# Later due times in a planned instruction order, and 64-row matmul operands padded to 128 rows

## The chip, the cores and the metric

The kernel runs on one core of one Trainium2 chip. The metric is device time in microseconds (us), the median over the runs shown. The core has a matmul engine (TensorE; PE in the rows, its weight loads PEld), VectorE (DVE), ScalarE (ACT), GpSimd (POOL) and SyncE (SP), which issues nearly all DMAs here. Each engine takes its instructions in the order in which the program lists them, and a waiting instruction holds up those behind it on its engine.

## The reference, cut

One step of an encoder with two layers, for a prompt of 512 rows and a sample of 64 rows with a model width of 2048. The two are laid side by side as T = 576 rows: four and a half blocks of 128. Layer 0 has two branches, A and B, that share one input projection; layer 1 is an attention with two softmax maps per head. Everything is float32.

```python
def ab_layer(x, ...):                                    # layer 0
    u, v_a, g_a, h_b, g_b = split(x @ w_in)
    v_n = layer_norm(v_a)                                # branch A
    out_a = u * spatial_gate(v_n, a_ws, a_bs) * silu(g_a)      # lower-triangular mixing in chunks of 128 rows
    hs = h_b + (prev - h_b) * b_mu                       # branch B; prev = h_b one row earlier
    r, k, v, wl, al = split(hs)
    decay = exp(-exp(-softplus(-(b_w0 + tanh(wl) @ b_w2)) - 0.5))
    a = sigmoid(b_a0 + al @ b_a2)
    ...
    wkv_new, y = rwkv7_scan(wkv0, r, decay, k_mod, v, kk, a)   # 16 heads of 64
    out_b = (group_norm(y) + sum(r * k_mod * b_rk) * v) * silu(g_b)
    return layer_norm(ALPHA * x + concat([out_a, out_b]) @ w_out)

def step(s, inp):                                        # rwkv7_scan, one row
    s_kk = einsum('bhvk,bhk->bhv', s, kk_t)
    s = s * w_t - s_kk * (kk_t * a_t)^T + v_t * k_t^T    # state of 64 x 64 per head
    return s, einsum('bhvk,bhk->bhv', s, r_t)

def c_layer(x, k_cache, v_cache, ...):                   # layer 1; the sample reads 512 cached rows too
    q, k, v, g = split(x @ w_in)
    attn = softmax(q1 k1) - lam * softmax(q2 k2)
    return layer_norm(ALPHA * x + (sub_norm(attn @ v) * silu(g)) @ w_out)
```

## The kernel before, in words

**Projections.** Most of the matmul work is `x @ w_in` and `x @ w_out` of both layers, cut into units of 128 output columns (`run_unit`). Numbers are split into a high and a low part, so that each product takes three matmuls (L280 to L282): high weights by high x, high weights by low x, low weights by high x. `x_...` is a tile of x, `wh` and `wl` are the parts of the weights, `p` the result. Weights come in by DMAs of 256 KB on the SP queue (L207, `w_dma`); ACT makes `wh` (L221), DVE or POOL `wl` (L223).

**Side work.** All else is written as generators that run beside the projections. A planner, `Flow`, walks through the program before it is built and counts an assumed time: each triple of projection matmuls adds 3 x columns / 2.35 ns (327 ns for 256 columns, 408 ns for 320). A generator yields two numbers, the time that its matmuls take and a delay; it is called again at the first triple at which the planner's time has passed the delay:

```python
    def step(self, h):
            pe_ns, lat = next(h[1])
            self.t += pe_ns
            h[0] = self.t + lat
    def tick(self, ns):
        self.t += ns
        for h in list(self.sides):
            if h in self.sides and h[0] <= self.t:
                self.step(h)
```

So a delay decides how many projection matmuls stand between two pieces of side work. It sets an order for every engine and no time: at run time an instruction waits for its operands where it stands.

**Branch B** runs in 8 groups of two heads (groups 1 to 8 in the text, `g` = 0 to 7 in the code). `prepare` makes the decays (`sig`, L692, cumulated L716, `EP` and `EN`), `av` (L698), `rn` (L726, L727) and `rkm` (L735). `rwkv` makes `AR` and `KB` (DVE, L749 to L753) and their products per chunk of 64 rows (L773, `MM`), and turns the group's old state `st` (L796). The blocks on the diagonal of `MM` are inverted on DVE in 72 small tiles (L813): they reach this form by a store and a load (`ND`, `NT`), and the result `XX` and its transposed form go back by a store (`XD`, L820 and L821) and two loads each into `X16` and `V16` (L825; X and V in the rows). `stepmm` (L647) takes `X16` first, then `V16`, and builds the remaining inverse `ZB`.

**The chain of states.** The state goes through the 9 chunks in 8 steps (the first takes two chunks at once). One step, a link, is: PE L860 (`cq` from `VU`, `MM`), ACT copies `R1` (L864), PE L867 (`R1`, `ZB`), DVE copies to `VU` (L870), PE L873 (`VU`, `KB`), DVE makes the next `VU` (L881 or L883), which the next L860 needs. After the chain come the outputs `yq` (L896, L900) and `normalise` (L913 to L941), which scales them with `L162` out of the transposes of `yd` (L929).

**64-row operands.** The sample makes the fifth block of rows half full. Where a matmul or a transpose contracts over the rows of such a block, or over one head's 64, it takes 64 rows of the array: `to_features` (L189) for x, for the norm between the layers (`z`) and for the attention's output (`O`); `vn` (L471), `av` (L698), `sig` (L716), `st` (L796), and in layer 1 `aTs` (L1370) and `ovs` (L1381).

Of the kernel before, what the change touches and what calls it, by code (L numbers as in the profile page):

```python
# [10 lines left out]
F32 = mybir.dt.float32  # L11
# [106 lines left out]
def hybrid_step(ctx: ExitStack, tc: tile.TileContext, a: dict, o: list):  # L118
# [64 lines left out]
    def to_features(src, part, f0, m0=0):  # L183

        q = ps("tf")
        c = 0
        for m in MP[part]:
            n = rows(m)
            pe.transpose(q[:, c:c + n], src[:n, m - m0, f0:f0 + 128], ident[:n, :n])  # L189
            c += n  # L190
        return q[:, 0:c]

# [201 lines left out]
    with tc.tile_pool(name="xld", bufs=4) as xlp:  # L394
# [49 lines left out]
        def gated(j):  # L444
            vt = ap_.tile([128, 5, 128], F32, tag="at", name="vn")
            gb = ap_.tile([128, 3, 128], F32, name="gb")
            sp.dma_start(out=vt[:, 0:4, :], in_=VD[j][:, 0:4, :])
            sp.dma_start(out=vt[:64, 4, :], in_=VD[j][:64, 4, :])
# [18 lines left out]
            for ms in MP:  # L467
                q = ps()
                for i, m in enumerate(ms):
                    n = rows(m)  # L470
                    pe.matmul(q[:, 128 * i:128 * i + n], vt[:n, m, :], WST[:n, g, 0:n], start=True, stop=True)  # L471
                c0 = 128 * ms[0]
                dve.tensor_tensor(out=gt[:, c0:c0 + 256].rearrange("p (m t) -> p m t", m=2),
                                  in0=q[:, 0:256].rearrange("p (m t) -> p m t", m=2),
                                  in1=gb[:, 2:3, :].to_broadcast([128, 2, 128]), op=ALU.add)
                if len(ms) == 3:
                    dve.tensor_tensor(out=gt[:, 512:576], in0=q[:, 256:320], in1=gb[:, 2, 0:64], op=ALU.add)
                yield 110 * len(ms), 0
# [92 lines left out]
    WA = lp.tile([128, T], F32, name="WA")  # L571
    TW = lp.tile([65, T], F32, name="TW")
    pool.memset(TW[64:65, :], 1.0)

    def ev_shift(j, part, p):
# [81 lines left out]
    def rwkv_loads(g):  # L657
        w2 = r2p.tile([128, 2, 128], F32, name="w2")
        sp.dma_start(out=w2[0:64, 0, :], in_=a["ab_b_w2"][0, :, 128 * g:128 * g + 128])
        sp.dma_start(out=w2[64:65, 0, :], in_=a["ab_b_w0"][0:1, 128 * g:128 * g + 128])  # L660
        sp.dma_start(out=w2[64:128, 1, :], in_=a["ab_b_a2"][0, :, 128 * g:128 * g + 128])
        st = r2p.tile([64, 2, 64], F32, name="st")
        sp.dma_start(out=st, in_=a["state_b_wkv"][0, 0, 2 * g:2 * g + 2].rearrange("h v k -> v h k"))
        LOADS[g] = (w2, st)
# [17 lines left out]
    def prepare(g):  # L682
# [6 lines left out]
        for m in range(5):  # L689
            n = rows(m)  # L690
            q = q0[:, 128 * m:128 * m + 128] if m < 4 else q1[:64, 0:128]
            pe.matmul(q, TW[:, 128 * m:128 * m + n], w2[0:65, 0, :], start=True, stop=True)  # L692
        act.activation(out=sig[:, 0:4, :], in_=q0.rearrange("p (m f) -> p m f", m=4), func=AF.Sigmoid)
        act.activation(out=sig[:64, 4, :], in_=q1[:64, 0:128], func=AF.Sigmoid)
        av = fp.tile([128, T], F32, tag="f", name="av")
        for c0, c1 in TP:
            q = ps()
            pe.matmul(q[:, 0:c1 - c0], w2[64:128, 1, :], WA[64:128, c0:c1], start=True, stop=True)  # L698
            act.activation(out=av[:, c0:c1], in_=q[:, 0:c1 - c0], func=AF.Sigmoid, bias=A0[:, g:g + 1])
# [11 lines left out]
        for ms, ch in (((0, 1), (0, 4)), ((2, 3, 4), (4, 9))):  # L711
            q = ps()
            for i, m in enumerate(ms):
                n = rows(m)
# [24 lines left out]
    def rwkv(g):  # L739
# [117 lines left out]
        for cs in ((8, 0), (1,), (2,), (3,), (4,), (5,), (6,), (7,)):  # L857
# [16 lines left out]
            for c in cs:  # L874
# [155 lines left out]
    def z_tiles(zp, part, n=4):  # L1030
# [154 lines left out]
    def ev_v(hd, e, part, p):  # L1185
# [82 lines left out]
    def core(hd):  # L1268
# [74 lines left out]
        def sample_scores():  # L1343
            q0, q1 = ps("s0"), ps("s1")
            for j in range(2):
                pj = slice(64 * j, 64 * j + 64)
                pe.matmul(q0[pj, :], qT[j][:, 128:192], kcT[:, j, :], start=True, stop=True)
                pe.matmul(q1[pj, 0:64], qT[j][:, 128:192], kT[j][:, 512:576], start=True, stop=True)
            Pt = a2.tile([128, T], F32, tag="P", name="Ps")
            mx = a2.tile([128, 2], F32, name="mx")  # L1350
# [14 lines left out]
        def sample_values():  # L1365
            Pt, rr = st.pop("s")
            q = ps("aTs")
            for m in range(5):
                n = rows(m)
                pe.matmul(q[:n, 64 * m:64 * m + 64], Pt[:, 128 * m:128 * m + n], rr, start=True, stop=True)  # L1370
            aT = a1.tile([128, 2, 512], F32R, tag="aT", name="aTs")
            for n, cs in ((128, slice(0, 256)), (64, slice(256, 320))):
                dve.tensor_copy(aT[:n, 0, cs], q[:n, cs])
                dve.tensor_tensor(out=aT[:n, 1, cs], in0=q[:n, cs], in1=aT[:n, 0, cs].bitcast(F32), op=ALU.subtract)
            yield 5 * 150, 2800
            q = ps("ovs")
# [284 lines left out]
```

## Time and profile before

| | |
|---|---|
| runs | 2517.45, 2525.48 and 2527.79 us; median 2525.48 |
| profiled execution | 2536.78 us; span 2535.0 us, mean granted clock of TensorE 0.987 |
| busy, share of the span | PE 2433.9 us (96%), PEld 92%, DVE 52%, ACT 36%, POOL 20% |
| DMA | 281.71 MB, 111 GB/s over the span |
| chain that ended last | PE 81%, DVE 8%, DMA 8%, issue 2%, ACT 1%, SP's queue 1% |

The chain that ended last follows the work back from the last instruction to whatever released each step. "Busy" of a matmul includes time in which it stands in the pipeline behind another, so 96% does not say that 96% of the span is full use. A granted clock of 1.00 is 2.4 GHz and 0.50 is 1.2 GHz. Layer 0 is the first 1100 us of the span, roughly; branch B's groups lie in it.

### The profile page before, as it was taken

To read this page: it belongs to the slowest core of one execution; us is meant where nothing else is said; L and a number is where in the kernel's file an instruction comes from. 1 tells how busy PE (TensorE), PEld (TensorE's weight loads), DVE (VectorE), ACT (ScalarE), POOL (GpSimd) and SP (SyncE) were. 2 spreads that over 40 slices of the span, in tenths; PEclk is the share of its full clock that TensorE was granted. 3 is DMA by queue.
4 is the path that set the end of the run, shared out by engine and by line. 5 is a ranking of instruction groups with operands and counts; after the bars stand their busy time and mean duration, and the time that the engine had idled before them with its cause. 6 is when DMAs were issued, how large, how long until landed. Compare 5 with 4: busy or idle time off the path is not lost.

```text
span 2535.0 us, 48231 instructions
## 1 busy us (share of the span) xinstructions
PE 2433.9 (96%) x19033; PEld 2335.1 (92%) x19033; DVE 1327.7 (52%) x3030; ACT 904.1 (36%) x1827; POOL 517.2 (20%) x618
## 2 busy tenths in 40 slices
PE   8999898989898999999999999999999999999898
PEld 8988897979797988899999999999999999999897
DVE  4357465657474666556655434243333334356665
ACT  3424242414233231244434424243433433243342
POOL 1221212222221221121215121212021211213411
PEclk9999999999999999999999999999999999999998
DMA  6252424243342514267656242323233323337664
GB/s 178 71 96 60 80 70 78 75 72 86 57 91 54 104 48 90 91 214 220 189 159 181 84 120 81 102 85 107 85 103 89 97 88 98 102 92 231 186 184 148
DMA packets 528051, 281.71 MB, mean 111 GB/s; under 512 B 81288, under 2 KB 520010, under 8 KB 527818
## 3 DMA queue, kind: packets, MB, share of 16 engines
q1 hardware_dynamic: 527824, 278.63, 41.2%
q8 instruction: 149, 2.44, 0.4%
q14 instruction: 78, 0.64, 0.1%
HBM read 243.46 MB, written 35.09 MB: 110 GB/s over the span
## 4 chain that ended last, share of the span: by engine, by line
PE 81%; DVE 8%; DMA 8%; issue 2%; ACT 1%; SPq 1%; POOL 0%; DVEq 0%; ACTq 0%; POOLq 0%
PE p L280 22%; PE p L281 20%; PE p L282 20%; PE gps L647 2%; DMA ND<-MM 2%; DMA X<-XD 2%; DVE pr L813 2%; PE tt L178 1%; DVE wl L223 1%; PE cq L867 1%; PE cq L860 1%; PE tf L189 1%; DVE VU L883 1%; DMA r<-in_c_w_out 1%; PE p L249 1%
## 5 line engine op out<-in xcount | busy, mean ns | idle before, releaser
L280 PE MATMUL p<-x,wh 128*128 128x320 f32 (+1 forms) x4640 | 1435.9, 309 | 2.0 <-ACT wh L221 1.3
L282 PE MATMUL p<-x,wl 128*128 128x320 f32 (+1 forms) x4640 | 1383.1, 298 | 5.5 <-DVE wl L223 5.2
L281 PE MATMUL p<-x,wh 128*128 128x320 f32 (+1 forms) x4640 | 1381.8, 298 | 0.3 <-DVE x L168 0.2
L280 PEld LDWEIGHTS p<-x,wh 128*128 128x128 f32 x4640 | 884.2, 191 | 18.5 <-issue 3.5
L282 PEld LDWEIGHTS p<-x,wl 128*128 128x128 f32 x4640 | 883.0, 190 | 8.1 <-DVE wl L223 7.7
L281 PEld LDWEIGHTS p<-x,wh 128*128 128x128 f32 x4640 | 885.3, 191 | 1.2 <-DVE x L168 0.8
L223 DVE TENSOR_TENSOR wl<-r,wh 128x512 fp32r<-128x512 f32 x587 | 448.6, 774 | 436.0 <-ACT wh L221 427.6
L221 ACT CAST wh<-r 128x512 fp32r<-128x512 f32 x760 | 457.8, 620 | 476.1 <-PE p L281 321.9
L223 POOL TENSOR_TENSOR wl<-r,wh 128x512 fp32r<-128x512 f32 x173 | 232.8, 1346 | 889.3 <-ACT wh L221 709.8
L864 ACT COPY R<-cq 128x128 f32<-128x128 f32 x72 | 19.1, 265 | 225.1 <-PE cq L860 220.4
L249 PE MATMUL p<-wl,x 128*128 128x256 f32 x256 | 73.0, 285 | 1.4 <-DVE wl L223 1.1
L247 PE MATMUL p<-wh,x 128*128 128x256 f32 x256 | 72.6, 284 | 1.0 <-ACT wh L221 1.0
L248 PE MATMUL p<-wh,x 128*128 128x256 f32 x256 | 72.5, 283 | 0.0
L783 POOL TENSOR_TENSOR MM<-MM,CT 64x576 f32<-64x576 f32 x16 | 20.3, 1269 | 202.7 <-DMA ND<-MM 135.8
L1210 POOL TENSOR_TENSOR V<-vt,V 128x512 fp32r<-128x512 f32 (+1 forms) x32 | 27.3, 874 | 155.2 <-DVE V L1204 155.2
L870 DVE COPY VU<-cq 64x64 f32<-64x64 f32 x144 | 31.9, 222 | 50.6 <-PE cq L867 47.8
L813 DVE TENSOR_TENSOR pr<-XX,NT 72x1 f32<-72x1 f32 (+14 forms) x120 | 47.4, 395 | 18.5 <-DMA NT<-ND 15.1
L860 PE MATMUL cq<-VU,MM 128*128 128x128 f32 x144 | 30.9, 306 | 26.9 <-DVE VU L883 20.3
L860 PEld LDWEIGHTS cq<-VU,MM 128*128 128x128 f32 x144 | 21.2, 191 | 38.6 <-PE p L282 33.4
L840 DVE TENSOR_TENSOR Z<-gps,V 128x256 f32<-128x256 f32 (+1 forms) x32 | 14.5, 457 | 73.8 <-PE gps L647 73.8
L249 PEld LDWEIGHTS p<-wl,x 128*128 128x128 f32 x256 | 49.1, 192 | 2.3 <-DVE wl L223 2.2
L1169 POOL TENSOR_TENSOR qkv<-kT,qkv 128x256 fp32r<-128x256 f32 x32 | 25.2, 787 | 123.2 <-ACT qkv L1168 117.6
(379 smaller groups left out, 2599.1 us busy)
## 6 DMA issues: line engine op xcount, KB each, us to landing
r<-in_c_w_in SPq DMA_DIRECT2D x276, 256.0 KB
r<-in_ab_w_in SPq DMA_DIRECT2D x228, 256.0 KB
r<-in_ab_w_out SPq DMA_DIRECT2D x128, 256.0 KB
r<-in_c_w_out SPq DMA_DIRECT2D x128, 256.0 KB
t<-y SPq DMA_DIRECT2D x32, 160.0 KB
xt<-in_x_prompt SPq DMA_DIRECT2D x8, 512.0 KB
kc<-in_cache_c_k SPq DMA_DIRECT2D x16, 256.0 KB
out<-kt SPq DMA_DIRECT2D x16, 256.0 KB
```

Of the source, the lines that this page charges most:

```text
L221: act.copy(wh, r)
L223: eng.tensor_tensor(out=wl, in0=r, in1=wh.bitcast(F32), op=ALU.subtract)
L247: pe.matmul(hq[t], x[:, 0, ts], wh[:, kk, :], start=first, stop=False)
L248: pe.matmul(hq[t], x[:, 1, ts], wh[:, kk, :], start=False, stop=False)
L249: pe.matmul(hq[t], x[:, 0, ts], wl[:, kk, :], start=False, stop=bool(last))
L280: pe.matmul(out, wh[:, kk % 4, :], x[:, 0, :], start=(hp == 0 and kk == 0), stop=False)
L281: pe.matmul(out, wh[:, kk % 4, :], x[:, 1, :], start=False, stop=False)
L282: pe.matmul(out, wl[:, kk % 4, :], x[:, 0, :], start=False, stop=(hp == 1 and kk == 7))
L647: pe.matmul(q[HS[h], 64 * (c - c0):64 * (c - c0) + 64], L[h][HS[h], c, :], R[HS[h], c, :], start=True, stop=True)
L813: dve.tensor_tensor(out=pr[:, 0:t, 0:t], in0=XX[:, 0:t, 0:t].rearrange("p s j -> p j s"), in1=NT[:, 0:t, t:t + 1].rearrange("p s u -> p u ...
L860: pe.matmul(q[c][:, 0:128], MM[:, c, 0, :, :], VU[:, c, :, :], start=True, stop=True)
L870: dve.tensor_copy(VU[HS[h], c, h, :], q[c][HS[h], 128 + 64 * h:192 + 64 * h])
```

## The change

It has three parts. **Padding:** tiles whose fifth block had 64 rows get 128, POOL clears the padding (67 more instructions on POOL), and the matmuls take all 128 rows. **Links:** the delays behind the three pieces of a link go from 0, 500 and 200 ns to 450, 700 and 900. **Loads of the transposed matrix:** the delays from the store of `XD` to the loads and on to `stepmm` go from 3350 and 7600 ns (both tiles loaded together) to 5600 (`X16`), 2600 (`V16`) and 2200. Lines of the changed kernel stand 4 further down in branch B.

```diff
         for m in MP[part]:
-            n = rows(m)
-            pe.transpose(q[:, c:c + n], src[:n, m - m0, f0:f0 + 128], ident[:n, :n])
-            c += n
-        return q[:, 0:c]
+            pe.transpose(q[:, c:c + 128], src[:, m - m0, f0:f0 + 128], ident)
+            c += 128
+        return q[:, 0:TP[part][1] - TP[part][0]]
...
+            pool.memset(vt[64:128, 4, :], 0.0)
...
-                    pe.matmul(q[:, 128 * i:128 * i + n], vt[:n, m, :], WST[:n, g, 0:n], start=True, stop=True)
+                    pe.matmul(q[:, 128 * i:128 * i + n], vt[:, m, :], WST[:, g, 0:n], start=True, stop=True)
...
+        pool.memset(w2[0:64, 1, :], 0.0)
...
-        st = r2p.tile([64, 2, 64], F32, name="st")
+        st = r2p.tile([128, 2, 64], F32, name="st")
+        pool.memset(st[64:128, :, :], 0.0)
...
-            pe.matmul(q, TW[:, 128 * m:128 * m + n], w2[0:65, 0, :], start=True, stop=True)
+            pe.matmul(q, TW[:, 128 * m:128 * m + 128], w2[0:65, 0, :], start=True, stop=True)
...
-            pe.matmul(q[:, 0:c1 - c0], w2[64:128, 1, :], WA[64:128, c0:c1], start=True, stop=True)
+            pe.matmul(q[:, 0:c1 - c0], w2[:, 1, :], WA[:, c0:c1], start=True, stop=True)
...
-                pe.matmul(q[:, 130 * i:130 * i + w], sig[:n, m, :], TRI[:n, 0:w], start=True, stop=True)
+                pe.matmul(q[:, 130 * i:130 * i + w], sig[:, m, :], TRI[:, 0:w], start=True, stop=True)
...
-        pe.transpose(q[:, 0:64], st.rearrange("p h k -> p (h k)"), ident[:64, :64])
+        pe.transpose(q[:, 0:128], st.rearrange("p h k -> p (h k)"), ident)
...
-        yield 0, 3350
-        for d, x in zip(XD, (X16, V16)):
+        for d, x, ns in zip(XD, (X16, V16), (5600, 2600)):
+            yield 0, ns
             for h in range(2):
                 sp.dma_start(out=x[HS[h]], in_=drows(d, h))
-        yield 0, 7600
+        yield 0, 2200
...
-            yield 218 * len(cs), 0
+            yield 218 * len(cs), 450
...
-            yield 218 * len(cs), 500
+            yield 218 * len(cs), 700
...
-            yield 218 * len(cs), 200
+            yield 218 * len(cs), 900
...
+                pool.memset(VT[hd][64:128, 4, :, :].bitcast(F32), 0.0)
...
+        pool.memset(O[64:128, 4, :], 0.0)
...
-                pe.matmul(q[:n, 64 * m:64 * m + 64], Pt[:, 128 * m:128 * m + n], rr, start=True, stop=True)
+                pe.matmul(q[:, 64 * m:64 * m + 64], Pt[:, 128 * m:128 * m + 128], rr, start=True, stop=True)
...
-                three(q[:64, 0:256], aT[:n, 0, cs], aT[:n, 1, cs], (v[:, 0, :], v[:, 1, :]), m == 0, m == 4)
+                three(q[:64, 0:256], aT[:, 0, cs], aT[:, 1, cs], (v[:, 0, :], v[:, 1, :]), m == 0, m == 4)
```

Since delays set the order, the rows of the order show what moved. First PE in a chain of states: a link's L867 (`R1` by `ZB`) to the next link's L860. Before:

```order
L867 MATMUL cq<-R_6312,ZB 128x128
L280 MATMUL p<-x_199,wh 128x256
L281 MATMUL p<-x_199,wh 128x256
L282 MATMUL p<-x_199,wl 128x256
L280 MATMUL p<-x_208,wh 128x256
L281 MATMUL p<-x_208,wh 128x256
L282 MATMUL p<-x_208,wl 128x256
L873 MATMUL cq<-VU,KB 128x128
L280 MATMUL p<-x_217,wh 128x256
L281 MATMUL p<-x_217,wh 128x256
L282 MATMUL p<-x_217,wl 128x256
L860 MATMUL cq<-VU,MM 128x128
```

Of the change, the last piece alone, from a link's third matmul (now L877) to the next link's first (now L864):

```order
L877 MATMUL cq<-VU,KB 128x128
L280 MATMUL p<-x_251,wh 128x320
L281 MATMUL p<-x_251,wh 128x320
L282 MATMUL p<-x_251,wl 128x320
L280 MATMUL p<-x_262,wh 128x320
L281 MATMUL p<-x_262,wh 128x320
L282 MATMUL p<-x_262,wl 128x320
L280 MATMUL p<-x_278,wh 128x320
L281 MATMUL p<-x_278,wh 128x320
L282 MATMUL p<-x_278,wl 128x320
L864 MATMUL cq<-VU,MM 128x128
```

Three projection matmuls stood there before and nine do now. In the same way six instead of three follow a link's first matmul, and six to nine instead of six its second.

Then the SP queue in group 3, from the last store of branch A's `vt` to the loads of `X16` (X) and `V16` (V). Before:

```order
L451 DMA gb<-in_ab_a_bs 128x128
L423 DMA vd_143<-vt 128x256
L425 DMA vd_143<-vt 64x128
L207 DMA r<-in_ab_w_in 128x4x128
L825 DMA X_700<-XD_698 64x9x64 x2
L825 DMA V_701<-XD_699 64x9x64 x2
```

Of the change:

```order
L453 DMA gb<-in_ab_a_bs 128x128
L424 DMA vd_147<-vt 128x256
L426 DMA vd_147<-vt 64x128
L207 DMA r<-in_ab_w_in 128x4x128 x2
L829 DMA X_705<-XD_703 64x9x64 x2
L829 DMA V_706<-XD_704 64x9x64 x2
```

In groups 1 and 3 one more weight load stands ahead of X. In groups 2 and 4 to 8 two stood there before and two do now; only V has in some of them one more DMA ahead of it.

Last DVE, in group 6, where `prepare` and `rwkv` make `rkm` and `AR` for the next products and the group before is normalised (`y`, `yd`). Before:

```order
L940 TENSOR_TENSOR y_7783<-y_7783,hs 128x576
L941 TENSOR_TENSOR y_7783<-y_7783,gs 128x576
L223 TENSOR_TENSOR wl<-r,wh 128x512 x2
L726 TENSOR_SCALAR rn<-rn 128x256
L727 RECIPROCAL rn<-rn 128x256
L726 TENSOR_SCALAR rn<-rn 128x320
L727 RECIPROCAL rn<-rn 128x320
L730 SCALAR_TENSOR_TENSOR rn<-hs,VA,rn 128x576
L732 SCALAR_TENSOR_TENSOR av<-rn,av 128x576
L735 SCALAR_TENSOR_TENSOR rkm<-hs,VA,km 128x576
L223 TENSOR_TENSOR wl<-r,wh 128x512 x2
L749 TENSOR_TENSOR AR<-rn,EP 128x9x64
```

Of the change:

```order
L730 TENSOR_SCALAR rn<-rn 128x256
L731 RECIPROCAL rn<-rn 128x256
L730 TENSOR_SCALAR rn<-rn 128x320
L731 RECIPROCAL rn<-rn 128x320
L734 SCALAR_TENSOR_TENSOR rn<-hs,VA,rn 128x576
L736 SCALAR_TENSOR_TENSOR av<-rn,av 128x576
L739 SCALAR_TENSOR_TENSOR rkm<-hs,VA,km 128x576
L162 TENSOR_SCALAR y_7929<-gps,VA 64x4x64
L162 TENSOR_SCALAR y_7929<-gps,LXS 64x4x64 x2
L162 TENSOR_SCALAR y_7929<-gps,VA 64x4x64
L223 TENSOR_TENSOR wl<-r,wh 128x512
L753 TENSOR_TENSOR AR<-rn,EP 128x9x64
```

The scaling of the group before (L162, four instructions) stood far ahead of `rkm` and stands now between `rkm` and `AR`; its last two products (L940, L941) come behind `AR`.

## Rows read from the trace of the kernel before

**Rows 1.** The page, its first two parts: the span, the busy time and instructions of the matmul engine PE, and the granted TensorE clock in 40 slices of the span (tenths of full speed).

```profile
span 2535.0 us, 48231 instructions
PE 2433.9 (96%) x19033; PEld 2335.1 (92%) x19033; DVE 1327.7 (52%) x3030; ACT 904.1 (36%) x1827; POOL 517.2 (20%) x618
...
PEclk9999999999999999999999999999999999999998
```

**Rows 2.** Who waited for whom, of PE and (last row) of its weight loads PEld: us in total, times, longest us.

```profile
PE gps L647 <- DMA X<-XD: 21.4, 13, 4.9
PE cq L860 <- DVE VU L883: 20.3, 47, 1.1
PE cq L873 <- DVE VU L870: 8.3, 8, 1.7
...
PE cq L860 <- DVE VU L881: 6.5, 8, 0.8
...
PEld cq L867 <- ACT R L864: 16.6, 59, 0.5
```

**Rows 3.** The timeline of PE in two short stretches (start us, us, engine, line, operation, tiles, rows*columns of the array and shape). First the 64-row transpose of `st` between two matmuls of the projection; then two full 128-row transposes in the same place.

```profile
848.74 0.28 PE L282 MATMUL p<-x,wl 128*128 128x256 f32 x1
848.95 0.27 PE L796 MATMUL gps<-ident,st 64*128 64x64 f32 x1
849.15 0.39 PE L280 MATMUL p<-x,wh 128*128 128x256 f32 x1
849.37 0.28 PE L281 MATMUL p<-x,wh 128*128 128x256 f32 x1
...
1815.19 0.31 PE L282 MATMUL p<-x,wl 128*128 128x320 f32 x1
1815.33 0.38 PE L189 MATMUL tf<-ident,O 128*128 128x128 f32 x2
1815.47 0.39 PE L280 MATMUL p<-x,wh 128*128 128x320 f32 x1
1815.70 0.31 PE L281 MATMUL p<-x,wh 128*128 128x320 f32 x1
```

**Rows 4.** Groups of instructions by shape, of PE: three of the operations that the change pads (line, operation, tiles, rows*columns and shape, count | busy us, mean ns of one | idle before).

```profile
L189 PE MATMUL tf<-ident,xt 64*128 64x64 f32 x16 | 4.4, 273 | 0.0
...
L698 PE MATMUL gps<-WA,w 64*128 64x320 f32 x16 | 5.6, 429 | 0.0
...
L796 PE MATMUL gps<-ident,st 64*128 64x64 f32 x8 | 2.2, 272 | 0.0
```

**Rows 5.** The timeline of one link of the chain of states, in group 8: PE and VectorE (DVE) rows; in brackets the idle time before, and what ended it.

```profile
1019.46 0.46 PE L860 MATMUL cq<-VU,MM 128*128 128x128 f32 x2 [0.34 <-DVE VU L883]
...
1019.68 0.39 PE L280 MATMUL p<-x,wh 128*128 128x320 f32 x1
1019.91 0.31 PE L281 MATMUL p<-x,wh 128*128 128x320 f32 x1
1020.05 0.31 PE L282 MATMUL p<-x,wl 128*128 128x320 f32 x1
1020.33 0.49 PE L867 MATMUL cq<-R,ZB 128*128 128x128 f32 x2
...
1021.44 0.49 PE L873 MATMUL cq<-VU,KB 128*128 128x128 f32 x2
...
1021.97 0.60 DVE L883 SCALAR_TENSOR_TENSOR VU<-cq,EC,SE 64x64 f32<-64x64 f32 x2 [0.58 <-PE cq L873]
...
1022.71 0.46 PE L860 MATMUL cq<-VU,MM 128*128 128x128 f32 x2 [0.34 <-DVE VU L883]
```

**Rows 6.** Group 6 around the transposed matrix: the DMA queue's (SP) timeline; then PE's; then, from the chain of work that ended last in order of time, how long the second load of `X16` took from issue to landing (start us, us) in group 3 and in group 6.

```profile
753.04 3.16 SPq L207 DMA_DIRECT2D r<-in_ab_w_in  x2
756.30 1.28 SPq L825 DMA_DIRECT2D X<-XD  x2
...
760.67 0.31 PE L282 MATMUL p<-x,wl 128*128 128x320 f32 x1
762.62 0.32 PE L647 MATMUL gps<-X,MM 64*64 64x64 f32 x2 [1.63 <-DMA X<-XD]
...
403.21 4.34 DMA X<-XD
...
756.99 6.34 DMA X<-XD
```

**Rows 7.** Busy time of each engine in 10 us behind the wait for the transposed matrix, in groups 2 and 4; the column behind POOL is the granted clock (1.00 is 2.4 GHz, 0.50 is 1.2 GHz).

```profile
283.00:293.00 10.00, 5.91 (x76) 5.30 (x78) 0.29 (x1) 1.42 (x3) 1.32 (x2) 0.66 0.66 138
...
525.00:535.00 10.00, 8.22 (x125) 7.26 (x125) 1.87 (x5) 1.42 (x3) 1.32 (x2) 0.83 0.56 109
```

**Rows 8.** The timeline from the end of one group's outputs (L900) to the next group's first products (L773): the two PE rows and the DVE rows between that the prediction speaks of.

```profile
920.84 1.27 PE L900 MATMUL yq<-VU,MM 128*64 128x64 f32 x36
...
931.97 0.54 DVE L162 TENSOR_SCALAR y<-gps,VA 64x256 f32<-64x256 f32 x1 [2.24 <-PE gps L929]
...
954.73 0.76 DVE L753 TENSOR_TENSOR AR<-hs,EP 128x576 f32<-128x576 f32 x1
...
957.59 0.60 PE L773 MATMUL gps<-AR,KB 64*128 64x128 f32 x6
```

**Rows 9.** The memset of `ZB` by the POOL engine (count | busy us, mean ns).

```profile
L627 POOL MEMSET ZB<- 128x1152 f32 x1 | 1.1, 1062 | 0.0
```

More of the change, by code (lines that the diff above doesn't have):

```diff
@@ L308, in x_load @@
         if part:
+            pool.memset(xt[64:128, 2, :], 0.0)
             sp.dma_start(out=xt[:64, 2, :], in_=xs_ap[:, cs])
@@ L571, in hybrid_step @@
     WA = lp.tile([128, T], F32, name="WA")
-    TW = lp.tile([65, T], F32, name="TW")
+    TW = lp.tile([65, T + 64], F32, name="TW")
     pool.memset(TW[64:65, :], 1.0)
+    pool.memset(TW[0:64, T:], 0.0)
     def ev_shift(j, part, p):
@@ L661, in rwkv_loads @@
         sp.dma_start(out=w2[64:128, 1, :], in_=a["ab_b_a2"][0, :, 128 * g:128 * g + 128])
-        st = r2p.tile([64, 2, 64], F32, name="st")
-        sp.dma_start(out=st, in_=a["state_b_wkv"][0, 0, 2 * g:2 * g + 2].rearrange("h v k -> v h k"))
+        st = r2p.tile([128, 2, 64], F32, name="st")
+        pool.memset(st[64:128, :, :], 0.0)
+        sp.dma_start(out=st[0:64, :, :], in_=a["state_b_wkv"][0, 0, 2 * g:2 * g + 2].rearrange("h v k -> v h k"))
         LOADS[g] = (w2, st)
@@ L689, in prepare @@
         for m in range(5):
-            n = rows(m)
-            q = q0[:, 128 * m:128 * m + 128] if m < 4 else q1[:64, 0:128]
-            pe.matmul(q, TW[:, 128 * m:128 * m + n], w2[0:65, 0, :], start=True, stop=True)
+            q = q0[:, 128 * m:128 * m + 128] if m < 4 else q1[:, 0:128]
+            pe.matmul(q, TW[:, 128 * m:128 * m + 128], w2[0:65, 0, :], start=True, stop=True)
         act.activation(out=sig[:, 0:4, :], in_=q0.rearrange("p (m f) -> p m f", m=4), func=AF.Sigmoid)
-        act.activation(out=sig[:64, 4, :], in_=q1[:64, 0:128], func=AF.Sigmoid)
+        act.activation(out=sig[:, 4, :], in_=q1[:, 0:128], func=AF.Sigmoid)
         av = fp.tile([128, T], F32, tag="f", name="av")
@@ L713, in prepare @@
             for i, m in enumerate(ms):
-                n = rows(m)
                 w = 130 if m < 4 else 65
-                pe.matmul(q[:, 130 * i:130 * i + w], sig[:n, m, :], TRI[:n, 0:w], start=True, stop=True)
+                pe.matmul(q[:, 130 * i:130 * i + w], sig[:, m, :], TRI[:, 0:w], start=True, stop=True)
             nch = ch[1] - ch[0]
@@ L1035, in z_tiles @@
         pool.memset(zmv[part], 1.0)
+        if part and n == 4:
+            pool.memset(zt[part][64:128, 2, :], 0.0)
     P = {}
@@ L1348, in sample_scores @@
                 pe.matmul(q1[pj, 0:64], qT[j][:, 128:192], kT[j][:, 512:576], start=True, stop=True)
-            Pt = a2.tile([128, T], F32, tag="P", name="Ps")
+            Pt = a2.tile([128, T + 64], F32, tag="P", name="Ps")
+            pool.memset(Pt[:, T:], 0.0)
             mx = a2.tile([128, 2], F32, name="mx")
@@ L1368, in sample_values @@
             for m in range(5):
-                n = rows(m)
-                pe.matmul(q[:n, 64 * m:64 * m + 64], Pt[:, 128 * m:128 * m + n], rr, start=True, stop=True)
+                pe.matmul(q[:, 64 * m:64 * m + 64], Pt[:, 128 * m:128 * m + 128], rr, start=True, stop=True)
             aT = a1.tile([128, 2, 512], F32R, tag="aT", name="aTs")
-            for n, cs in ((128, slice(0, 256)), (64, slice(256, 320))):
-                dve.tensor_copy(aT[:n, 0, cs], q[:n, cs])
-                dve.tensor_tensor(out=aT[:n, 1, cs], in0=q[:n, cs], in1=aT[:n, 0, cs].bitcast(F32), op=ALU.subtract)
+            cs = slice(0, 320)
+            dve.tensor_copy(aT[:, 0, cs], q[:, cs])
+            dve.tensor_tensor(out=aT[:, 1, cs], in0=q[:, cs], in1=aT[:, 0, cs].bitcast(F32), op=ALU.subtract)
             yield 5 * 150, 2800
@@ L1377, in sample_values @@
             for m in range(5):
-                n = rows(m)
                 cs = slice(64 * m, 64 * m + 64)
-                v = VC[m] if m < 4 else V[:64, 4]
-                three(q[:64, 0:256], aT[:n, 0, cs], aT[:n, 1, cs], (v[:, 0, :], v[:, 1, :]), m == 0, m == 4)
+                v = VC[m] if m < 4 else V[:, 4]
+                three(q[:64, 0:256], aT[:, 0, cs], aT[:, 1, cs], (v[:, 0, :], v[:, 1, :]), m == 0, m == 4)
             act.activation(out=O[:64, 4, :], in_=q[:64, 0:256], func=AF.Square, accum_out=ss[:64, 4:5])
```

## The prediction

> **What bounds the kernel now.** I read the page first: PE is busy for 2433.9 of 2535.0 us and the granted clock is at nine tenths or more in all but the last slice [rows 1]. So only what PE executes, or idles for, moves the end. Over 19033 instructions the busy time is 0.128 us each. The waits of PE come next. Two kinds are large: `stepmm` on the transposed matrix X, 21.4 us in 13 waits, and the chain of states: L860 on the next `VU`, 20.3 and 6.5 us; L867's weight load on ACT's copy, 16.6 us; L873 on DVE, 8.3 us [rows 2]. Then I read the timeline where the edits are. A link of the chain [rows 5] goes round in 1022.71 - 1019.46 = 3.25 us. PE has little to do in it: its own product takes 0.22 us until the projection begins, the three projection matmuls 0.23, 0.14 and (by the second) 0.14, together 0.73, three times over 2.19. About 1.06 us of each link is lost, and three projection matmuls between L873 and L860 (0.5 us) cannot hide the way through DVE, which ends 1022.57 - 1021.44 = 1.13 us after L873 starts. Since PE does the same projections in any order, each lost us that is filled is won at the end.
>
> **Padding.** A 64-row transpose between projection matmuls: from L282 to the second matmul behind it 849.37 - 848.74 = 0.63 us. With two 128-row transposes in the same place the distance is 0.51 [rows 3]; one transpose fewer (0.07) and projections of 256 instead of 320 columns (0.03 each for two) make it 0.38. So going to 64 rows and back costs 0.25 us, 0.28 if the exit's bubble too scales with the width; I take 0.27. The instructions themselves (273, 429 and 272 ns mean, pipelined [rows 4]) become no dearer by rows: the two full transposes of rows 3 stand 0.14 us apart. Stretches that fall away: 48 of L189 (16 each for x, `z` and `O`), and 8 each for `av`, `sig`, `st`, `vn` and `aTs`: 88 x 0.27 = 23.8 us. Some 12 of them (`st` and half of `vn`) lie between L773 and a `stepmm` that waits for X anyway; 12 x 0.27 = 3.2 goes into that wait. `ovs` keeps an output of 64 columns and I count nothing for it. **-21 us**, bounds -8 (the other stretches are partly hidden) and -30 (0.34 a stretch, by the 0.21 us that stand between L282 and the transpose in rows 3 where 0.14 do for full rows).
>
> The 67 POOL instructions: `ZB`'s memset of 1152 elements takes 1062 ns [rows 9], 0.92 ns an element. By that 8 each of 128 (`vn`, `w2`, `st`), 512 (`V`), 256 (`O`) and 64 (`Ps`), and a few for x and `z`, come to some 14 us on POOL, which does other work while PE multiplies; they stand far ahead of their readers. Nothing, and 14 us if every one delayed a reader.
>
> **Links.** By the order there are nine projection matmuls in place of three ahead of L860, six for three ahead of L867, six to nine for six ahead of L873. Nine last 3 x 0.51 = 1.5 us, over the 1.13 that DVE needs; three more ahead of L867 add at least 0.4, over the 16.6 / 59 = 0.28 that its weight load waits now [rows 2]. Ordinary links are covered. What is there to win: 8 groups of 8 links lose 64 x 1.06 = 68 us, and the 8.3 of L873 fall in links where a unit's end puts its evacuation and a weight's split ahead on DVE, so not in the link of rows 5: 76 gross. The bare waits of rows 2, 20.3 + 6.5 + 16.6 + 8.3 = 51.7, leave out the refilling behind a wait. What stays: these 8 stalls have 1.04 us each and get up to three matmuls (0.43) more: 5 us. The same stall will meet the two other pieces of a link as often, where the longer spacing has just enough cover for a free DVE: 16 x 0.9 = 14. 76 - 19 = 57; **-56 us**, bounds -30 (half of the gross is lost to unit ends) and -72.
>
> **Loads of the transposed matrix.** The planner's delays say X is loaded later and `stepmm` comes 10950 - 10400 = 550 ns earlier. What counts is the SP queue. In groups 2 and 4 to 8 the order ahead of X is the same two weight loads, so X goes out when they do: SP reaches them at 753.04, X at 756.30, and PE, done at about 761, idles 1.63 us until 762.62 [rows 6]. X's landing therefore stays, and PE gets there earlier: 0.55 us by the delays, and by the 12 stretches, 1.5 a group, 0.4; so the wait grows by 0.9 x 8 = 7 us. In groups 1 and 3 one more weight load stands ahead of X; X landed 4.34 us after its issue with one ahead (group 3) and 6.34 with two (group 6) [rows 6], so 2 more each: 4 us. Behind these waits the clock falls: 10 us behind the wait in group 2 have 0.66 of full clock, in group 4 0.83 [rows 7], that is 3.4 and 1.7 us lost. A longer wait may lengthen that: 2 us, an estimate from the difference of these two. **+13 us**, bounds -36 (waits of 21.4 and dips of about 15, the mean of rows 7, 2.55, in six groups, all vanish) and +25 (the 2 us of rows 6 more in six groups).
>
> **Next in line: `AR`.** Links with 1.35 us more delay each push the end of a chain some 9 us later against the next group's `prepare`, which keeps its time. Before, 36.7 us lie from L900 to the next L773, and DVE's scaling of `y` (L162, 0.54 each) is over at 932, long before `AR` (954.73, 0.76), which ends 2.1 us before L773 [rows 8]. In the changed order four L162, 4 x 0.54 = 2.2 us, stand between `rkm` and `AR`. That eats the 2.1, and L773 (L777 of the change) will wait for DVE wherever a weight's split also falls in between: 1 us in each of 8 groups, **+8 us**, bounds 0 and +16.
>
> **The sum** is -21 - 56 + 13 + 8 = -56 us against the profiled execution's own 2536.78 (span 2535.0 and 1.8 around it): 2481. The runs' median lies 11.3 lower, so **2469 us**.
>
> **Rivals.**
> - *X's wait and the clock dips vanish*, because the loads' later place lets them go out behind other traffic without queueing: C is -36 instead of +13, 2420 us. For it: 21.4 us is the largest wait, and this part of the change can only aim there. Against: the SP rows ahead of X are unchanged in six groups and worse in two. Chance 0.15.
> - *Unit ends eat half of the link's gain*: the excess moves from L860 to L867 and L873, since all three depend on ACT and DVE, whose queues do not change. B is -28: 2497 us, and up to 2513 if `AR` costs its 16 too. For it: L873 already waits 1.04 us at a time with six matmuls in front. Chance 0.17.
> - *Slower: the chain becomes the bound.* Each group's chain is 9 us longer; if the next group's L773 then waits for DVE, which still normalises, by more than the whole gain, (21 + 56 - 13) / 8 = 8 us a group, the kernel is no faster; at 10 us a group, 2542. Against: DVE would have to be 10 us behind where it was 2.1 ahead, and only 2.2 us of work have moved in front of `AR`. Chance 0.04.
> - *The padding gives nothing*: A is 0, 2490 us, if 64-row operands run beside their neighbours and full rows take that away. Rows 3 speak against it: the 64-row transpose starts 0.21 us behind L282, the full ones 0.14 and 0.14 apart. Chance 0.04.
>
> The Trainium skill bears on the last rival: "TensorEngine Tiling (Array Packing)", Overview, promises up to twice the speed for a contraction of 64 or less, since a second tile of the array works beside the first; by that rule padding would take away a gain, and the sum would be -35. The same page, Tiling Modes, says that changing the mode drains the engine; the 0.63 us of rows 3 agree with this second rule, and there no second 64-row tile works beside `st`.
>
> **How the numbers follow.** The forecast has 0.60, with its own range 2440 to 2492 (each term half way to its bounds, partly cancelling). The range 2425 to 2500 leaves out most of the first rival (0.10), the tail of the second (0.06) and the third (0.04). A measurement of this kernel tells about 0.5% (12.6 us) from nothing: under 2513 is faster. Slower comes from the third rival, 0.03; within 0.5% from its lower half and the tail of the second, 0.04; faster 0.93.
>
> **What would show it.** Right: PE's waits at the links' first product (now L864) under 5 us where they were 26.8, L871's weight load under 6 where 16.6, L877 about as before or a little more; no 64-row form left at L189, `st` and `av`; the wait for X at 25 to 33 us; a new wait of PE for `AR` of 5 to 10. Wrong in the first place if X's wait falls below 15, for then its time was set by something else than the two weight loads; in the second if the links' waits stay above 25 together; in the padding if the distance from L282 over `st` stays at 0.6.

## The result and the profile after

The changed kernel takes 2557.47 us (median of 4 runs, 2552.73 to 2562.77) against 2521.57 of the kernel before beside it: 1.0141 times as long, 95% interval 1.0107 to 1.0175. The forecast was 2469 us, and "slower" had a chance of 0.03. The profiled execution took 2555.21 us; its mean granted clock is 0.972 where it was 0.987. The page of the changed kernel:

```profile
span 2553.4 us, 48262 instructions
PE 2418.6 (95%) x19033; PEld 2356.3 (92%) x19033; DVE 1321.3 (52%) x3014; ACT 893.7 (35%) x1821; POOL 528.2 (21%) x672
```

Against [rows 1] PE is busy for 15 us less in a span that is 18.4 longer. The waits of PE, then one row of the waits of its weight loads (us in total, times, longest us); lines stand 4 further down than before:

```profile
PE gps L651 <- DMA X<-XD: 34.5, 15, 8.8
PE p L282 <- DVE wl L223: 30.3, 15, 4.1
PE gps L933 <- DVE yd L927: 16.9, 6, 2.8
PE p L282 <- POOL wl L223: 7.9, 5, 1.9
...
PE cq L877 <- DVE VU L874: 4.0, 13, 1.5
...
PE cq L864 <- DVE VU L887: 2.6, 8, 1.0
...
PEld cq L871 <- ACT R L868: 4.9, 10, 0.5
```

Against [rows 2] the links did what was forecast: L864 waits 2.6 us where L860 waited 26.8, L871's load 4.9 where 16.6, L877 4.0 where 8.3. Together 51.7 became 11.5. X's wait rose from 21.4 to 34.5, a little over the 25 to 33 forecast. Nearly half of that rise, 6 us, falls in groups 2 and 3, where PE now comes to `stepmm` 6.2 and 6.5 us after the issue of `XD`'s store and came 9.4 and 10.5 us after it before; the forecast had PE come 0.9 us earlier in all groups. Two rows have no counterpart of size in the profile before: the low parts of the weights, 30.3 and 7.9 us where DVE's stood at 5.2, and `yd`, 16.9. The forecast had put 8 us on `AR` in that place, and there is no wait of PE for `AR`.

A link of group 8, PE's timeline, to be read beside [rows 5] (the first row belongs to the first step, which takes two chunks, hence x4): nine projection matmuls lie between the first two rows and six between the last two, and no idle time.

```profile
1050.50 0.61 PE L877 MATMUL cq<-VU,KB 128*128 128x128 f32 x4
...
1052.27 0.46 PE L864 MATMUL cq<-VU,MM 128*128 128x128 f32 x2
...
1053.29 0.39 PE L871 MATMUL cq<-R,ZB 128*128 128x128 f32 x2
```

L877 to L864 takes 1.77 us, all of it filled; L864 to L871 1.02. The padding, beside [rows 3], is seen over `st` (L800, now 128 rows, lies between the two rows):

```profile
259.02 0.28 PE L282 MATMUL p<-x,wl 128*128 128x256 f32 x1
...
259.37 0.28 PE L281 MATMUL p<-x,wh 128*128 128x256 f32 x1
```

0.35 us where 0.63 stood, in each of the eight groups; the forecast had worked out 0.38 for full rows.

**Where the time went.** By L900 (now L904) the chain of group 7 ended 11.5 us ahead of group 8's first `sig` (L692, now L697) before (920.84 in [rows 8], and the first row here), and 3.7 us after it in the changed kernel (the other two rows): 15.2 us later, where the forecast had put some 9.

```profile
932.32 1.42 PE L692 MATMUL gps<-w,TW 65*128 65x128 f32 x10
...
956.61 1.28 PE L697 MATMUL gps<-w,TW 65*128 65x128 f32 x10
...
960.30 1.27 PE L904 MATMUL yq<-VU,MM 128*64 128x64 f32 x36
```

So the normalisation of one group and `prepare` of the next now run through ACT and DVE side by side. ACT, then POOL, DVE and PE, in that stretch of the changed kernel:

```profile
969.75 0.46 ACT L724 ACTIVATE EN<-gps 128x320 f32<-128x320 f32 x1
970.22 1.28 ACT L925 ACT_TABLE_LOAD   x1
971.52 0.30 ACT L925 ACTIVATE va__10549<-va__10549,EPS 128x9 f32<-128x9 f32 x1
...
970.34 2.88 POOL L756 TENSOR_TENSOR KB<-km,EN 64x576 f32<-64x576 f32 x2 [4.88 <-issue]
...
968.21 0.75 DVE L924 TENSOR_REDUCE va__10549<-y 128x9 f32<-128x576 f32 x1
971.86 0.21 DVE L926 RECIPROCAL va__10549<-va__10549 128x9 f32<-128x9 f32 x1 [2.90 <-ACT va__10549 L925]
972.10 1.73 DVE L927 TENSOR_TENSOR yd<-yd,va__10549 128x576 f32<-128x576 f32 x1
...
973.89 0.76 PE L933 MATMUL gps<-ident,yd 128*128 128x128 f32 x5 [2.75 <-DVE yd L927]
```

The sums `va_` are there at 969, but ACT serves the next group's exponentials first (L724), loads a table (1.28 us) for the square root (L925), and DVE idles 2.90 us for it. `yd` is done at 973.8, and PE has waited 2.75 us for it. Some 1 us of that comes from `yd`'s own product: it takes 1.73 us here and took 0.76 before. In all seven groups of the changed kernel in which it takes 1.67 us or more, POOL's `KB` (L756) runs beside it for 1.1 us; in the eighth, and in all eight groups before, nothing runs on POOL and it takes 0.76. No run puts `KB` elsewhere to test this. From there DVE has no pause until 983.3 (`rn`, `rkm`, the scalings L162), and then, DVE and PE:

```profile
983.33 0.69 DVE L223 TENSOR_TENSOR wl<-r,wh 128x512 fp32r<-128x512 f32 x1
983.94 0.75 DVE L753 TENSOR_TENSOR AR<-rn,EP 128x576 f32<-128x576 f32 x1
984.61 1.51 DVE L755 TENSOR_TENSOR KB<-av,EN 64x576 f32<-64x576 f32 x2
...
987.01 2.19 DVE L768 COPY VU<-gps 64x256 f32<-64x256 f32 x6
989.12 0.67 DVE L223 TENSOR_TENSOR wl<-r,wh 128x512 fp32r<-128x512 f32 x1
...
989.85 0.58 PE L282 MATMUL p<-x,wl 128*128 128x256 f32 x1 [4.07 <-DVE wl L223]
```

ACT has cast the weights' high part by 984.5. The low part (the second L223) stands behind `AR`, `KB` and `VU` on DVE, 5.2 us of work, and PE idles 4.07 us in the middle of a projection. Both waits come in groups 2 and 4 to 8, with 2.75 to 2.83 us for `yd` and 2.98 to 4.09 us for the low part. And nearly all of these holes, idle stretches of PE, bring the clock down. Here are the 10 us that begin with the same wait in group 6 (the column behind POOL is the granted clock; the rows of groups 2 and 4 before are [rows 7], whose windows hold their wait too):

```profile
736.00:746.00 10.00, 5.93 (x33) 5.39 (x33) 7.65 (x16) 0.07 (x1) 0.00 (x0) 0.68 0.48 137
```

By the trace's record of the clock, 28 stretches at half clock (143.3 us in all, PE busy in 117.7 of them) stand where 12 did (70.2 and 53.1). Half of PE's work in them is taken as lost: (117.7 - 53.1) / 2 = 32 us, an estimate. The links gave 40 us by waits and some 45 by the distances of PE's instructions: from a chain's first L860 to its last, the time less 0.147 us for each projection matmul of 320 columns and 0.120 for each of 256 is 115 us over the eight groups before and 70 in the changed kernel. In sum: X +13, low parts +33, `yd` +17, clock +32, links -45, padding about -25 (88 x 0.28): +25, where the spans differ by 18; the rest is small and overlaps (a wait for `vn` is 4 us shorter, and part of the spacing behind a wait runs at half clock).

### The profile page after: what moved, and what is told of

The parts are those of the page before. It is cut to its first block, busy times and chain, and to the rows that moved or that the text cites. A ratio compares the mean times of both kernels' runs of the same rounds, so it can differ in the third digit from the quotient of the medians.

```text
span 2553.4 us, 48262 instructions
## 1 busy us (share of the span) xinstructions
PE 2418.6 (95%) x19033; PEld 2356.3 (92%) x19033; DVE 1321.3 (52%) x3014; ACT 893.7 (35%) x1821; POOL 528.2 (21%) x672
## 4 chain that ended last, share of the span: by engine, by line
PE 76%; DVE 11%; DMA 6%; issue 4%; ACT 2%; POOL 1%; SPq 0%; DVEq 0%; ACTq 0%; POOLq 0%
PE p L280 20%; PE p L282 20%; PE p L281 20%; DVE wl L223 2%; DMA X<-XD 2%; PE gps L651 2%; PE tt L178 1%; DVE rn L731 1%; PE tf L189 1%; PE gps L777 1%; ACT wh L221 1%; DMA r<-in_ab_w_out 1%; PE cq L877 1%; PE p L249 1%; DMA XD<-XX 1%
## 5 line engine op out<-in xcount | busy, mean ns | idle before, releaser
L282 PE MATMUL p<-x,wl 128*128 128x320 f32 (+1 forms) x4640 | 1393.6, 300 | 38.4 <-DVE wl L223 30.3
L282 PEld LDWEIGHTS p<-x,wl 128*128 128x128 f32 x4640 | 892.0, 192 | 43.3 <-DVE wl L223 33.7
L223 DVE TENSOR_TENSOR wl<-r,wh 128x512 fp32r<-128x512 f32 x587 | 442.6, 762 | 437.0 <-ACT wh L221 420.1
L223 POOL TENSOR_TENSOR wl<-r,wh 128x512 fp32r<-128x512 f32 x173 | 236.5, 1367 | 805.1 <-ACT wh L221 680.8
L160 ACT ACTIVATE tm<-p,VA 128x256 f32<-128x256 f32 (+1 forms) x50 | 25.2, 504 | 87.7 <-PE p L282 84.2
L651 PE MATMUL gps<-X,MM 64*64 64x64 f32 x288 | 18.3, 289 | 34.6 <-DMA X<-XD 34.5
L247 PEld LDWEIGHTS p<-wh,x 128*128 128x128 f32 x256 | 49.1, 192 | 1.3 <-ACT wh L221 1.3
L651 PEld LDWEIGHTS gps<-X,MM 64*64 64x64 f32 x288 | 15.8, 196 | 37.3 <-issue 33.6
```

The costliest lines, as they stand in the source:

```text
L223: eng.tensor_tensor(out=wl, in0=r, in1=wh.bitcast(F32), op=ALU.subtract)
L247: pe.matmul(hq[t], x[:, 0, ts], wh[:, kk, :], start=first, stop=False)
L282: pe.matmul(out, wl[:, kk % 4, :], x[:, 0, :], start=False, stop=(hp == 1 and kk == 7))
L651: pe.matmul(q[HS[h], 64 * (c - c0):64 * (c - c0) + 64], L[h][HS[h], c, :], R[HS[h], c, :], start=True, stop=True)
```

## Experiments

Three theories. **1**: the links' due times push the end of a chain onto the next group's `prepare`. **2**: the loads' due times carry the loss. **3**: the padding does. A fourth came up later, **rival 4**: the denser chain itself makes DVE late, whatever the normalisation does. Ratios are to runs of the kernel before beside them.

**Padding alone.**

```diff
-            yield 218 * len(cs), 450      # and 700, 900
+            yield 218 * len(cs), 0        # and 500, 200
-        for d, x, ns in zip(XD, (X16, V16), (5600, 2600)):
+        yield 0, 3350                     # both tiles, then 7600
```

> The padding alone, with all due times as before; the order is the old one. Theory 1 (the links' due times are to blame: they push the end of a group's chain onto the next group's prepare) and theory 2 (the loads' due times are to blame) both expect the 21 us of the forecast's sum: about 2500 us, 2493 to 2508, no 64-row transposes of x, z and O left, the waits on the weights' low parts (L282 on L223) at 5 us as before. Theory 3 (the padding itself costs, by its memsets or longer matmuls): 2521 us or more, with POOL later in the waits.

2500.3 us, 0.9913 (0.9896 to 0.9931): 21 us. Theory 3 falls. PE's waits:

```profile
PE gps L651 <- DMA X<-XD: 13.9, 13, 3.1
...
PE p L282 <- DVE wl L223: 5.0, 7, 2.4
```

X's wait is 7.5 us shorter than in [rows 2], where the forecast let it grow by 3. X goes out on SP up to 2.1 us sooner behind its store (8.9 us after it instead of 11.0 in group 3, 5.9 as before in group 6); whether the padding does that, or the one profiled execution before, which was 15 us above the median of its kernel, these runs don't tell.

**Links alone.** On the kernel before:

```diff
-            yield 218 * len(cs), 0        # 500, 200
+            yield 218 * len(cs), 450      # 700, 900
```

> The links' due times alone (450, 700, 900), the rest as before. Theory 1: slower than before, 2535 to 2575 us; PE waits for yd (L929 on DVE) 10 us or more and for the weights' low parts (L282 on L223, DVE and POOL) 20 us or more, as in the changed kernel, with some ten half-clock stretches more, though the links' own waits are nearly gone. Theory 2: the 50 us that the links gain come out whole, 2465 to 2480 us, and those waits stay at 5 us.

2551.57 us, 1.0112 (1.0097 to 1.0127): 30 us slower by this edit alone. Theory 2 falls as the main cause:

```profile
PE p L282 <- DVE wl L223: 33.3, 16, 4.1
PE gps L929 <- DVE yd L923: 20.4, 7, 5.8
```

**Loads alone.** On the kernel before, delays of 5600, 2600 and 2200 for 3350 and 7600.

> The due times of the transposed matrix's loads alone (5600, 2600, 2200), the rest as before. Theory 1: X's wait grows from 21.4 to 25 to 34 us, the rest stays: 2521 to 2535 us. Theory 2: this part carries the loss of the change, 2540 to 2565 us, with X's wait at 34 us or more.

2525.38 us, 1.0011 (0.9999 to 1.0024); X's wait 21.5 us. By itself the third edit costs next to nothing.

**Padding and links**, the loads as before:

> The change with the old due times of the loads (3350, 7600). Theory 1: the waits for yd and for the weights' low parts stay (10 us and 20 us or more), 2530 to 2560 us. Theory 2: 2445 to 2465 us, the forecast's sum without the loads.

2534.89 us, 1.0045 (1.0030 to 1.0060): 14 us over the kernel before, where -21 and +30 alone would make 9.

```profile
PE p L282 <- DVE wl L223: 32.5, 18, 4.1
PE gps L933 <- DVE yd L927: 23.0, 7, 6.1
PE gps L651 <- DMA X<-XD: 18.3, 12, 7.9
```

But the loads' due times, worth 4 us alone, make 22 to 24 on top of this (by the medians and by the ratios). The reason is on the SP queue. Group 6 in the changed kernel (SP, then PE):

```profile
776.30 0.43 SPq L824 DMA_DIRECT2D XD<-XX  x1
...
778.04 1.94 SPq L207 DMA_DIRECT2D r<-in_ab_w_in  x2
782.20 1.28 SPq L829 DMA_DIRECT2D X<-XD  x2
...
788.86 0.29 PE L651 MATMUL gps<-X,MM 64*64 64x64 f32 x2 [2.87 <-DMA X<-XD]
```

and in the kernel without the new load times:

```profile
765.31 0.43 SPq L824 DMA_DIRECT2D XD<-XX  x1
...
767.06 1.25 SPq L207 DMA_DIRECT2D r<-in_ab_w_in  x1
771.21 1.29 SPq L829 DMA_DIRECT2D X<-XD  x2
...
776.29 0.30 PE L651 MATMUL gps<-X,MM 64*64 64x64 f32 x2 [1.29 <-DMA X<-XD]
```

PE comes to `stepmm` 9.7 us after the store's issue in both (788.86 - 2.87 - 776.30 and 776.29 - 1.29 - 765.31), X goes out 5.9 us after it in both, and lands 12.6 us after it with two weight loads ahead and 11.0 with one. The links' delays had shifted the groups against the weight loads so that the old due times let X go behind one load in all groups; the new ones put a second one back in all of them. X's wait goes from 18.3 to 34.5 us, the mean clock from 0.978 to 0.972.

**A later normalisation.** Padding and links, and for groups 1 to 7:

```diff
-        yield 0, 3500
+        yield 0, 12000 if g < 7 else 3500
         dve.tensor_reduce(out=va_, in_=y2, axis=AX.X, op=ALU.add)
```

> Padding and the links' due times (as e4_pad_links, 2535 us), and the first delay of the normalisation of groups 1 to 7 raised from 3500 to 12000 ns, so that its square root on ACT, yd and the four scalings stand behind the next group's AR on DVE; nothing else moves by design. Theory 1 (the longer chain pushes the normalisation into the next group's prepare, and PE waits there): the waits for yd (23.0 us) and for the weights' low parts (32.5 and 7.9 us) fall below 5 and 15 us, half-clock time falls with them, 2450 to 2475 us. Rival 4 (the denser chain itself, or a shifted phase against the unit ends, makes DVE late whatever the normalisation does): yd's wait goes, the low parts' stays at 25 us or more, 2500 to 2535 us.

2526.19 us, 1.0023 (1.0008 to 1.0039): 9 us back by the medians, 6 by the ratios, where 60 to 85 were expected. A miss; the time lies in rival 4's range, but the waits are not its picture either:

```profile
PE gps L933 <- DVE yd L927: 38.4, 7, 6.1
...
PE p L282 <- DVE wl L223: 12.9, 14, 2.4
```

The low parts' wait fell from 40.4 to 17.5 us (with POOL's 4.6), and none of the 4 us holes behind `AR`, `KB` and `VU` is left: it was the normalisation's work on DVE that made the low parts late there. But `yd`'s wait rose from 23.0 to 38.4. The edit moved `yd` behind `AR`, `KB` and `VU` on DVE, and its transposes are due on PE by a delay of 4.2 us as ever. The same edit on the whole change:

> The whole change, with the normalisation's first delay raised from 3500 to 12000 ns for groups 1 to 7, as in e5_late_norm. Theory 1: the change's 2557 us fall by 60 to 85 to 2470 to 2497 us; the difference to e5_late_norm is what the loads' due times cost where two weight loads stand ahead of X instead of one: X's wait at 25 us or more against 10 to 18. Rival 4: 2520 to 2557 us.

2550.99 us, 1.0122 (1.0100 to 1.0144): 6 us back, within the noise, where 60 to 85 were expected, and again in rival 4's range. It is 25 us over the kernel above, with X's wait at 52.7 us instead of 22.5. A cost of the loads of about 22 is so seen a second time, though PE here also comes to `stepmm` earlier (6.7 us after the store's issue in groups 4 to 7, 7.8 to 10.5 above).

**Both delays of the normalisation later.** As e5, and

```diff
-        yield 0, 4200
+        yield 0, 9000 if g < 7 else 4200
         ob = y2.rearrange("p c j -> p (c j)")
```

> As e5_late_norm (2526 us), and the normalisation's second delay raised as well, from 4200 to 9000 ns for groups 1 to 7, so that the transposes of yd are due on PE behind the time at which DVE is through with AR, KB and yd. Theory 1, mended (e5 only moved the collision: yd then stood behind 6 us of AR and KB on DVE and PE waited 38.4 us for it, with half-clock time behind each wait): the wait for yd falls below 8 us, that for the low parts stays near 17, and 40 to 60 us come back, 2466 to 2490 us. Rival 4: another wait of the same size takes its place (AR, MM or the low parts at 35 us or more), 2510 to 2530 us.

2498.18 us, 0.9904 (0.9882 to 0.9926): 28 us back where 40 to 60 were expected, 8 us above the range of theory 1 and 12 below that of rival 4. PE's waits, then DVE and PE in group 7:

```profile
PE gps L651 <- DMA X<-XD: 23.4, 15, 7.7
PE p L282 <- DVE wl L223: 20.9, 16, 2.4
PE gps L933 <- DVE MM L780: 7.2, 6, 1.4
...
812.78 0.81 DVE L739 SCALAR_TENSOR_TENSOR rkm<-hs,VA,km 128x576 f32<-128x576 f32 x1
813.51 1.28 DVE L223 TENSOR_TENSOR wl<-r,wh 128x512 fp32r<-128x512 f32 x2
...
814.25 0.39 PE L282 MATMUL p<-x,wl 128*128 128x256 f32 x1 [2.24 <-DVE wl L223]
```

Of `yd`'s own wait 2.1 us are left; 7.2 us came back behind `MM`. The low parts keep 20.9: in six groups, 12.6 us in all, they stand behind `rn`, `av` and `rkm` of the next group's `prepare` (L730 to L739) on DVE. So two delays of the normalisation, which do no work, are worth 37 us. The links' later due times had cost 35 us over the padding alone although the chains gained some 45, so 80 in all, and more than half of that is still lost: against the padding alone X waits 9.5 us more, the low parts 16.7 and the transposes of `yd` 9.3, at a mean clock of 0.986 instead of 0.992.

**One weight load fewer ahead of X there** (2700 and 8250 ns):

> As e9_late_norm2, and the loads of the transposed matrix 650 ns earlier (2700 and 8250 for 3350 and 7600), so that one weight load instead of two stands ahead of X on SP in groups 4 to 8. Theory 1 with the SP queue as the cause of X's wait: 10 to 15 us under e9_late_norm2, X's wait below 10 us, about 2460 us. If X's wait is set elsewhere: as e9_late_norm2 within 4 us.

2488.30 us, 0.9869 (0.9846 to 0.9892), X's wait 15.8 us: 10 us under the last one, as expected by difference (the intervals just overlap), but the wait was not under 10; 9.3 us of it fall in groups 2 and 3.

**Lateness alone.** Padding, the old links, and ahead of the first link

```diff
+        yield 0, 10800
         decayed(8)
```

> Padding, the links' old due times, and one delay of 10800 ns (8 x 1350, what the change adds in its links) ahead of a group's first link, so that the chain is as tight as before and only ends as late as in e4_pad_links. Theory 1 (lateness alone is the cause): the waits of e4 for yd and for the weights' low parts appear, 15 to 30 us and 30 us or more, while the links' own waits stay at 50 us: 2540 to 2590 us against 2500 of e1_padding. Rival 4 (the wider links themselves put DVE's work where it hurts): 2500 us within 10, those waits at 0 and 5 us.

2599.12 us, 1.0306 (1.0282 to 1.0330): 99 us over the padding alone, 9 more than the upper end expected. L900 (here L905) starts 3.7 us after the next group's first `sig`, as it does in the kernel with padding and links. Lines stand one further down:

```profile
PE gps L934 <- DVE yd L928: 49.6, 7, 7.9
PE cq L865 <- DVE VU L888: 29.3, 46, 1.7
...
PE p L282 <- POOL wl L223: 7.4, 5, 2.0
...
PE p L282 <- DVE wl L223: 5.4, 9, 2.4
```

No link is wider here than before, and the wait for `yd`, which here stands behind the next group's `rn` on DVE, is larger than in any other run. That lateness by itself does harm of this size is shown, and the wait for POOL's low parts comes with it (7.4 us; 7.9 in the change). That DVE's low parts wait too is not: they stay at 5.4 (5.0 with the padding alone), so their 30 us in the change hang on where exactly DVE's blocks come to stand, and rival 4 keeps that part.

**Half of the links' delay.** Padding, 225, 600 and 550:

> Padding, and half of the links' added delays (225, 600, 550 for 450, 700, 900); loads as before. The chain ends about half as much later. Theory 1: the links' own waits fall by half or more, to 25 us, and the collision with the next prepare is met in part only: 2470 to 2520 us, the waits for yd and the low parts between those of e1_padding (0 and 5 us) and e4_pad_links (23 and 40 us). Rival 4 has no step at a given lateness and expects the mean of the two, about 2517.

2492.41 us, 0.9892 (0.9870 to 0.9915): 8 us under the padding alone by the medians, 5 by the ratios, whose intervals overlap; not the mean of the two. The last outputs (L904) still start 7.4 to 9.5 us ahead of the next group's first `sig`, and there is no wait for `yd`; the links' L864 waits 12.7 us, but X 25.0.

**Earlier X.** Padding alone, 2000 and 8950 ns:

> Padding alone, with both loads of the transposed matrix 1350 ns earlier (2000 and 8950 for 3350 and 7600), so that one weight load fewer stands ahead of X on SP in six of the groups, and stepmm where it was. If the SP queue sets X's wait: 13.9 us (e1_padding) fall to 5 or less and two or three half-clock stretches go, 2480 to 2492 us against 2500. If X's way through memory sets it, whatever is ahead: 2497 to 2503 us.

2486.80 us, 0.9870 (0.9842 to 0.9897), 13.5 us under the padding alone:

```profile
PE gps L651 <- DMA X<-XD: 6.9, 11, 2.4
```

**Both**, the fastest kernel of the study:

> As e7_half_links (2492 us: padding, half of the links' added delays), and both loads of the transposed matrix 1350 ns earlier, as in e8_early_x, which takes away one or two weight loads ahead of X in every group. By e8's gain (13.5 us at an X wait of 13.9) and X's wait of 25.0 here: 2465 to 2480 us, with X's wait below 10 us. If the half links' gain and the early X were the same time counted twice: 2485 us or more.

2473.48 us, 0.9815 (0.9797 to 0.9833), with a mean clock of 0.993 and X's wait at 11.5 us. Against the early X without the links' delays the ratio falls from 0.9870 to 0.9815, 13 us and clear of both intervals: half of the links' delay is a gain. X's wait was not under 10 as expected; 5.7 us of it fall in group 3.

## Why the prediction was wrong

The step that failed is the term `AR`: it priced one reader of DVE's queue, where other readers were met.

- *Padding, -21*: right; 21 us by itself, and 0.28 us a stretch over `st` against the 0.27 taken. That X's wait fell in that run, where 3 us of the padding were to go into it, the forecast did not have. The clearing on POOL (54 memsets and 16.7 us in the trace, where 67 and some 14 were counted) shows up in no wait of size.
- *Links, -56*: what the links themselves give was nearly right (waits 51.7 to 11.5; 45 by distances), the net was not: alone, the edit costs 30 us, so some 75 came back.
- *Loads, +13*: X's wait grew by 13.1, but the reason given covered part of it: in groups 4 to 7 PE comes about 0.9 us earlier as forecast, in groups 2 and 3 three to four. The forecast compared the SP order of the change with that before and found it the same in six groups, which is right. It missed that the links alone take one weight load out from ahead of X there, which the third edit then put back. As an edit on top of the others it costs 22 us.
- *`AR`, +8*: the step that failed. The text saw that the four scalings had moved between `rkm` and `AR`, and priced only the 2.1 us of slack in front of L773. In its place the runs showed 33 us of waits for the low parts, 17 for `yd`, and half-clock time behind them; PE never waited for `AR`. The chain also ended 15.2 us later against `prepare`, not some 9 (and the scalings of [rows 8], "over at 932", began there and ended at 934.2). It did not follow the other readers of the same queues: ACT, where the square root and its table load came behind the next group's exponentials, with `yd` behind it; and the weights' low parts, which stand in DVE's queue and feed the projection itself. It named the split only as what would make `AR` late, when PE waits for the split. The third rival had the mechanism (the chain's end against the next group) but looked for the wait at L773 alone, where it would have needed 10 us a group, and gave it 0.04.
- *The clock*: the forecast allowed 2 us for longer half-clock time, only behind X. It cost some 32, since nearly every new hole is followed by some, as [rows 7] had shown for X.
- *The last rival*: that the padding gives nothing was wrong, by 0.63 to 0.35 us over `st` and by 21 us for the kernel. The rule of the Trainium skill, "TensorEngine Tiling (Array Packing)", Overview, would have made padding worthless or worse; these two numbers stand against it here, where no second 64-row tile has work beside `st`. The rule of the Trainium skill in Tiling Modes of the same page, that a change of mode drains the engine, agrees with both numbers.

What stays open: why X's wait fell with the padding alone, why PE comes to `stepmm` so much sooner in groups 2 and 3, how much of the low parts' wait is lateness and how much the place in DVE's queue, and what `KB` on POOL costs `yd`.

## What to carry to other kernels

A delay added to a chain that runs beside other work lengthens the chain, and what must be priced is whom its end meets: list every row that newly stands ahead of another on every engine, and price the wait of each reader, that of the main loop's own operands first. A wait that was removed here paid only where the work behind it did not land on a busier stretch; half of the added delay gave a gain (13 us, with the early X) where the whole gave a loss. Due times of several edits act together, so that the order has to be compared for pairs of them, not only for the whole and the start.

## What the runs showed of the hardware

In the changed kernel 22 of the 23 holes of 2 us or more in PE's work held the start of a stretch at half clock or were followed by one within 2.2 us, and more of such stretches cost some 32 us of the change: about as much as the whole loss by its medians (36 us). A 0.30 us square root behind four exponentials and a switch between tables on ACT (1.28 us) kept DVE idle for 2.90 us, and PE waited 2.75 us for what followed. A table load stood ahead of that square root before as well (DVE waited 0.77 us for it in the same group), and the change has 89 in all where 95 stood: what cost time is the place and not the number. A product on DVE (`yd`) took 1.67 to 1.75 us where POOL's `KB` ran beside it for 1.1 us, and 0.76 elsewhere. Full-row transposes of half empty tiles take no longer than 64-row ones (272 ns mean both for `st`), and passing to 64 rows and back costs 0.28 us in each of the eight groups there.
